# Sums of squares for two RMS norms: from transposed tiles with GpSimd additions to rows with a ScalarE row sum

## The chip, the cores and the metric

The kernel runs on one core of a Trainium2 chip. The metric is the device time of one execution in microseconds, as the median of three runs. A profile of one execution shows the engines: PE (TensorE, matmuls; its weight loads are shown apart as PEld), DVE (VectorE), ACT (ScalarE), POOL (GpSimd) and SP (SyncE, which here only issues DMAs; its queue is written SPq).

## The reference, cut to what matters

One layer of a hybrid decoder block. The input `x` (512 tokens x 2048) is normalised and projected; the columns of the projection feed an S5 scan, a differential attention and a cross-attention into 256 memory tokens, which are normalised too. All three are gated, concatenated, projected, normalised and added to `x`.

```python
def rmsnorm(x, g):
    var = jnp.mean(x32 * x32, axis=-1, keepdims=True)
    return (x32 * lax.rsqrt(var + NORM_EPS) * g).astype(x.dtype)

h = rmsnorm(x, norm_pre[l])
proj = h @ w_in[l]                    # 2048 x 5120
u_s, g_s, q_d, k_d, v_d, g_d, q_x, g_x = jnp.split(proj, split_at, axis=-1)
...
mem_n = rmsnorm(mem, norm_mem[l])
kv = mem_n @ w_mem_kv
```

The change concerns the two `mean(x32 * x32)`: of the 512 rows of `x` and of the 256 rows of `mem`.

## The kernel before, in words

All weights come in chunks of 128 x 1024 numbers (512 KB). The matmuls run in a split form: each operand is a high part (`hi`, a rounded copy made on ACT) and a low part (`lo`, the difference, made on DVE), and each product takes three matmuls (`mm3`). For a chunk, `load` (line 110) issues the DMA into one of three `raw` buffers, `parts` (line 124) makes `whi` on ACT and `wlo` on DVE into one of two buffers each, and the chunk's function then issues 24 or more matmuls in four portions. The main loop (from line 1090) does, for chunk n: load chunk n + 2, split chunk n + 1, run the matmuls of chunk n.

Between the four portions of each chunk the loop calls what is registered for that place: `at_slot(n, f)` puts `f` behind a quarter of chunk n, so slot 6.25 is behind the first portion of chunk 7. Everything outside the weight products is placed with it. PE's instructions keep the order of the program (`pin`). On the other engines and on SP's queue a list scheduler may let a later instruction pass an earlier one that cannot start yet; from chunk 9 on, ACT and DVE work is kept behind the latest weight split (`After`, `marks`).

Chunks 0 to 7 are the first four column tiles of u (the S5 input), with the contraction running over chunks, so that the transposed input can arrive in pieces: chunk c uses k = 2c and 2c + 1. `h_pair(k)` (line 308) loads 128 x 2 x 512 numbers of x transposed (`xT`, three buffers), and makes the scaled high part `hhi` on ACT and the low part `hlo` on DVE. `h_square(k)` (line 321) squares the same `xT` on ACT, and for all but the first, adds the squares to `xss` on POOL (line 327). A fold on POOL (line 360) leaves 128 x 512. `column_scale` (line 161) sums that over the partitions with tiny matmuls against ones, and `rsqrt_mean` (line 157) turns the sums into `rcol`, one scale for each token with the tokens on partitions: a DVE multiply-add and a power on POOL (line 159). `row_broadcast` (line 169) makes four diagonal matrices on DVE and four matmuls on PE, and a copy puts the scale for every partition into `rb`. The outputs of u are multiplied by it (`evac_u`, tile `ut`), which frees the accumulators that chunk 8 needs.

The memory follows the same way at chunks 8 to 19: `mem_load` and `mem_split` make `mhi` and `mlo` from transposed `mem`, `mem_square` (line 276) squares on ACT and adds into `macc` on POOL (line 282), `mem_stats` folds twice (lines 285 and 286), `column_scale` gives `rm`, and `row_broadcast` gives `rmb`.

In the same stretch other work shares DVE and POOL: `discretise` (many small DVE operations on tiles `sm`, `tw`, `pwr`, `npwi`, `w`), `rotary_tables` (`posf`, `rtmp`), `diff_lambda` (`lp`), and `s5_products`, whose products `bp`, `pm` and `dp` run on POOL (lines 575 to 578) and DVE and are then used by PE in `s5_maps` and `s5_weights` (transposes at line 99, small matmuls into `ps_t`). Most instructions of ACT, DVE and SP carry line 71, that of the helper that records them, so they are told apart by their tiles.

Of the kernel before, what the change touches and what calls it, by code (L numbers as in the profile page):

```python
# [10 lines left out]
F32 = mybir.dt.float32  # L11
# [8 lines left out]
P = 128  # L20
# [34 lines left out]
def tile_hybrid_block(ctx: ExitStack, tc: tile.TileContext, a: dict, out: bass.AP):  # L55
# [5 lines left out]
    class After:  # L61
        """An engine whose instructions stay behind the latest split of a weight chunk."""

# [31 lines left out]
    def mm(*args, **kw):  # L95
        pin(pe.matmul(*args, **kw))  # L96
# [63 lines left out]

    def column_scale(col, sq, n):
        """(mean + eps)^-1/2 of the columns of sq, with the columns on partitions."""
        sp_ = psum("t")
        w = sq.shape[-1] // P
        for j in range(w):
            mm(sp_[:, j:j + 1], sq[:, j * P:(j + 1) * P], ones[:, 0:1], start=True, stop=True)
        rsqrt_mean(col, sp_[:, :w], n)

    def row_broadcast(dst, r, n, pool):
# [36 lines left out]
    def add_cols(src, js, rhs, nk, evac, n=SEQ):  # L206
        """Column tiles js of a product with the columns on partitions."""
        acc = {}
        nc_ = nk // 8
        for c in range(nc_):  # L210
            for i, j in enumerate(js):
                def f(wh, wl, c=c, i=i, j=j):
                    if c == 0:
                        acc[j] = psum("mm")
                    for kk in range(8):
                        k = c * 8 + kk
                        sl = slice(kk * P, (kk + 1) * P)
                        rh, rl = rhs(k)
                        mm3(acc[j][:, :n], wh[:, sl], wl[:, sl], rh, rl, k == 0, k == nk - 1)
                        if kk in (1, 3, 5):  # L220
                            yield
                    if c == nc_ - 1:
                        evac(i, acc[j])
                    yield
                chunks.append((src[j, c], f))

    def add_rows(src, nt, lhs, order, evac, tag="mm"):
        """A product with the tokens on partitions, 512 columns."""
        acc = {}
# [20 lines left out]

    # ------------------------------------------------------------ memory keys and values
    s5stack, mstack, hstack, prstack = ExitStack(), ExitStack(), ExitStack(), ExitStack()
# [4 lines left out]
    mlo = mp.tile([P, NK, NMEM], F32R, name="mlo")  # L257
    macc = mp.tile([P, 4, NMEM], F32, name="macc")
    rmb = mp.tile([P, NMEM], F32, name="rmb")
# [15 lines left out]

    def mem_square(i4):
        if i4 == 0:
            s.activation(macc, mem_raw[0], AF.Square)
        else:
            msq = mp.tile([P, 4, NMEM], F32, tag="sq", name="msq", bufs=2)  # L280
            s.activation(msq, mem_raw[i4], AF.Square)
            g.tensor_tensor(macc, macc, msq, ALU.add)

    def mem_stats():
        g.tensor_tensor(macc[:, 0:2, :], macc[:, 0:2, :], macc[:, 2:4, :], ALU.add)
        g.tensor_tensor(macc[:, 0, :], macc[:, 0, :], macc[:, 1, :], ALU.add)

# [15 lines left out]

    # ------------------------------------------------------------ h^T and the token scale
    xss = xp_.tile([P, 2, SEQ], F32, name="xss")
    h_raw = {}
# [13 lines left out]

    def h_square(k):
        if k == 0:
            s.activation(xss, h_raw[k], AF.Square)
        else:
            sq = mp.tile([P, 2, SEQ], F32, tag="sq", name="sq", bufs=2)
            s.activation(sq, h_raw[k], AF.Square)
            g.tensor_tensor(xss, xss, sq, ALU.add)

    def h_scales():
        v.tensor_scalar(r05, rcol, 0.5, None, ALU.mult)  # L330
        v.tensor_scalar(r04, rcol, 0.5 * (1.0 - LAMBDA_INIT), None, ALU.mult)

    # ------------------------------------------------------------ u
    def evac_u(j, acc):
# [21 lines left out]
    for i, n in enumerate((0, 0.75, 1.5, 2.25, 3, 3.75)):  # L356
        at_slot(n, lambda k=2 * i + 4: h_pair(k))
        at_slot(n + 0.25, lambda k=2 * i: h_square(k))
    at_slot(4.5, lambda: h_square(12))
    at_slot(4.75, lambda: (h_square(14), g.tensor_tensor(xss[:, 0, :], xss[:, 0, :], xss[:, 1, :], ALU.add)))  # L360
    at_slot(5.5, lambda: column_scale(rcol, xss[:, 0, :], D))
    at_slot(6.25, lambda: row_broadcast(rb, rcol, NT, mp))
    at_slot(10, h_scales)
    for i in range(4):
        at_slot(8.5 + 2 * i, lambda i=i: (mem_load(i), mem_split(i), mem_square(i)))
    at_slot(15.5, mem_stats)
    at_slot(17, lambda: column_scale(rm, macc[:, 0, :], D))
    at_slot(19, lambda: row_broadcast(rmb, rm, 2, mp))

# [4 lines left out]

    # ------------------------------------------------------------ gates and memory queries, kept in DRAM
    def evac_to(dst):
# [12 lines left out]

    # ------------------------------------------------------------ parameters of the S5 group  # L390
    s5 = {}
# [52 lines left out]
    def cmul(dst, src, n, by):  # L444
        """Powers dst.. (n of them) as the powers src.. times the power by."""
        d_, x_ = slice(dst, dst + n), slice(src, src + n)
# [9 lines left out]
    def discretise():  # L456
        """abar = exp(lambda dt) and its powers 0 to 4, (abar - 1) / lambda times the powers 0 to 3;
        with the signs that the stacked real and imaginary halves of a group want."""
        dtt = exact_exp(ldt, "dt")
# [46 lines left out]
        v.tensor_scalar(npwi, npwi, -1.0, None, ALU.mult)  # L506
        # abar^4, with a pair of groups on the partitions: magnitude, and turns negated
        r_, f_, tmp = small(), small(), small()
# [36 lines left out]

    # ------------------------------------------------------------ S5: what depends on the parameters alone, kept in DRAM
    pre = {}
# [12 lines left out]
    def s5_products(o):  # L560
        """B with the powers 0 to 3 and (abar - 1) / lambda, C with the powers 0 to 4; real parts of a group
        on the lower half of the partitions, imaginary ones on the upper half."""
        bc = pt("bc", [512], 2)
# [29 lines left out]
    def s5_weights(o):  # L593
        """Direct kernels of the lags 0 to 3 (D on lag 0)."""
        bp, dp, kz = pre["bp", o], pre["dp", o], pre["kz"][o % 2]
# [10 lines left out]

    # ------------------------------------------------------------ S5
    def s5_open():
# [17 lines left out]
    def s5_load(o):  # L626
        """Maps and output maps of an octet of groups."""
        sp = t512("sp", 2, (P, 1152))
# [3 lines left out]
    def s5_u(i, x):  # L632
        """u of two octets, the first or the second groups of their pairs."""
        if x == 0:
# [9 lines left out]
    def s5_toeplitz(i, x):  # L644
        """The direct kernels of two octets as Toeplitz blocks."""
        tm = s5["d"][i % 2]["tm"]
# [5 lines left out]
    def s5_angles(o):  # L652
        """Cosines and sines of the turns of abar^4 at each chunk."""
        cs = t512("cs", 2, (P, 2, 4, P))
# [17 lines left out]
    def s5_states(o):  # L672
        """The states at the end of a chunk, in steps: turned back, summed, turned forward, spread over the groups."""
        x, ub, us, (c_, s_) = s5["d"][o % 2]["x"], s5["ub"], oct_[o]["us"], oct_[o]["cs"]
# [34 lines left out]
    def s5_outputs(o):  # L709
        """y, and twice its GELU"""  # L710
        d, us = s5["d"][o % 2], oct_[o]["us"]
# [53 lines left out]

    # ------------------------------------------------------------ GLU of the S5 group
    S1 = len(chunks)
# [35 lines left out]

    # ------------------------------------------------------------ memory attention, beside v and g_d
    S2 = len(chunks)
# [88 lines left out]

    # ------------------------------------------------------------ differential attention
    S3 = len(chunks)
# [19 lines left out]
    def evac_k(h, acc):  # L916
        """The keys of either map, on both halves of the partitions."""
        t1_, t2_ = rotary(acc)
# [9 lines left out]
    def evac_q(h, acc):  # L928
        """Of either map, the high parts on one half of the partitions and the low parts on the other."""
        t1_, t2_ = rotary(acc)  # L930
# [71 lines left out]

    # ------------------------------------------------------------ output projection, post norm, residual
    S4 = len(chunks)
# [36 lines left out]

    # the last 512 columns: four chunks as before, four kept for a pass by token tiles; the last tile in halves
    pieces = [(tt, c0, w) for tt, c0, w in ((0, 0, 512), (1, 0, 512), (2, 0, 512), (3, 0, 256), (3, 256, 256))]
# [37 lines left out]

    # ------------------------------------------------------------ the program
    for i in range(9):
# [131 lines left out]
```

## Time and profile before

| | |
|---|---|
| time, median of 3 runs (lowest, highest) | 843.36 us (842.02, 843.72) |
| span of the profiled execution | 843.7 us (the page gives no other time for it) |
| PE busy | 813.4 us (96%), 4042 matmuls |
| PEld busy | 672.5 us (80%) |
| DVE busy | 563.3 us (67%) |
| ACT busy | 351.7 us (42%) |
| POOL busy | 105.1 us (12%), 87 instructions |
| DMA | 125.32 MB, mean 149 GB/s |

The page cuts the span into 40 slices of 21.1 us; a digit is the busy share of an engine in a slice in tenths. A timeline row gives the start, the duration, the engine, the operation with its output and inputs, the count if several were merged, and in brackets how long the engine was idle before it and what ended that. A row of groups gives the count, the busy time and the mean in ns. A matmul's duration overlaps the next one's, so PE's pace is read from starts, not from durations.

### The profile page before, as it was taken

To read this page: it belongs to the slowest core of one execution; us is meant where nothing else is said; L and a number is where in the kernel's file an instruction comes from. 1 tells how busy PE (TensorE), PEld (TensorE's weight loads), DVE (VectorE), ACT (ScalarE), POOL (GpSimd) and SP (SyncE) were. 2 spreads that over 40 slices of the span, in tenths; PEclk is the share of its full clock that TensorE was granted. 3 is DMA by queue.
4 is the path that set the end of the run, shared out by engine and by line. 5 is a ranking of instruction groups with operands and counts; after the bars stand their busy time and mean duration, and the time that the engine had idled before them with its cause. 6 is when DMAs were issued, how large, how long until landed. Compare 5 with 4: busy or idle time off the path is not lost.

```text
span 843.7 us, 10965 instructions
## 1 busy us (share of the span) xinstructions
PE 813.4 (96%) x4042; PEld 672.5 (80%) x4042; DVE 563.3 (67%) x1001; ACT 351.7 (42%) x589; POOL 105.1 (12%) x87
## 2 busy tenths in 40 slices
PE   8797978998999999999999999999999999999996
PEld 6686768887878788878888888888888888888885
DVE  5998798646788888885675455557988943232335
ACT  7522442433353544424334353445767633131321
POOL 2703564630000000000000000000100010000000
PEclk9998988999999999999999999999999999999998
DMA  8444545883645555427656322222223426222226
GB/s 293 159 177 135 202 139 193 263 266 97 183 117 162 164 146 170 118 100 237 212 174 236 104 88 75 88 88 93 82 76 111 140 79 221 100 100 99 96 105 249
DMA packets 59494, 125.32 MB, mean 149 GB/s; under 512 B 12592, under 2 KB 26032, under 8 KB 59312
## 3 DMA queue, kind: packets, MB, share of 16 engines
q1 hardware_dynamic: 59440, 124.61, 44.9%
q8 instruction: 32, 0.52, 0.3%
q14 instruction: 22, 0.18, 0.1%
HBM read 103.22 MB, written 21.36 MB: 148 GB/s over the span
## 4 chain that ended last, share of the span: by engine, by line
PE 78%; DVE 12%; DMA 4%; issue 3%; ACT 2%; SPq 1%; POOL 0%; DVEq 0%; POOLq 0%; ACTq 0%
PE ps_mm L96 65%; PE ps_s L96 7%; PE ps_t L96 4%; DMA raw<-in_w_in_a_dram 2%; DVE wlo L71 2%; DVE sm L71 2%; DVE hlo L71 2%; PE ps_t L99 1%; DVE mlo L71 1%; DMA sp<-sp_dr 1%; SPq L71 1%; DVE x L71 1%; DVE ra L71 1%; ACT whi L71 1%; DVE ut L71 1%
## 5 line engine op out<-in xcount | busy, mean ns | idle before, releaser
L71 DVE TENSOR_TENSOR wlo<-raw,whi 128x1024 fp32r<-128x1024 f32 (+1 forms) x135 | 168.6, 1250 | 174.9 <-ACT whi L71 174.2
L71 ACT CAST whi<-raw 128x1024 fp32r<-128x1024 f32 (+1 forms) x135 | 139.0, 1030 | 326.4 <-PE ps_mm L96 214.2
L96 PE MATMUL ps_mm<-hhi,wlo 128*128 128x512 f32 x512 | 202.5, 395 | 8.8 <-DVE wlo L71 8.8
L96 PE MATMUL ps_mm<-hhi,whi 128*128 128x512 f32 x512 | 204.6, 400 | 0.3 <-DVE ut L71 0.3
L96 PE MATMUL ps_mm<-hlo,whi 128*128 128x512 f32 x512 | 202.5, 396 | 1.7 <-DVE hlo L71 1.7
L96 PEld LDWEIGHTS ps_mm<-hhi,wlo 128*128 128x128 f32 x512 | 97.9, 191 | 30.5 <-DVE wlo L71 9.6
L96 PEld LDWEIGHTS ps_mm<-hlo,whi 128*128 128x128 f32 x512 | 97.9, 191 | 22.5 <-DVE hlo L71 3.1
L96 PEld LDWEIGHTS ps_mm<-hhi,whi 128*128 128x128 f32 x512 | 98.0, 191 | 21.1 <-DVE ut L71 0.7
L159 POOL TENSOR_TENSOR so<-so,neghalf 128x1 f32<-128x1 f32 x16 | 11.6, 724 | 355.4 <-DVE so L71 327.4
L96 PE MATMUL ps_mm<-whi,hhi 128*128 128x512 f32 x128 | 49.9, 390 | 0.0
L96 PE MATMUL ps_mm<-whi,hlo 128*128 128x512 f32 x128 | 49.9, 390 | 0.0
L96 PE MATMUL ps_mm<-wlo,hhi 128*128 128x512 f32 x128 | 49.9, 390 | 0.0
L96 PE MATMUL ps_mm<-whi,yshi 128*128 128x512 f32 (+1 forms) x112 | 43.9, 392 | 0.0
L96 PE MATMUL ps_mm<-wlo,yshi 128*128 128x512 f32 (+1 forms) x112 | 43.3, 387 | 0.0
L96 PE MATMUL ps_mm<-whi,yslo 128*128 128x512 f32 (+1 forms) x112 | 43.3, 386 | 0.0
L96 PEld LDWEIGHTS ps_mm<-whi,hlo 128*128 128x128 f32 x128 | 24.0, 188 | 5.1
L96 PEld LDWEIGHTS ps_mm<-whi,hhi 128*128 128x128 f32 x128 | 24.1, 188 | 4.7
L96 PEld LDWEIGHTS ps_mm<-wlo,hhi 128*128 128x128 f32 x128 | 24.0, 188 | 4.8
L71 DVE SCALAR_TENSOR_TENSOR hlo<-xT,cols,hhi 128x512 fp32r<-128x512 f32 x16 | 25.1, 1610 | 2.9 <-ACT hhi L71 2.9
L71 DVE TENSOR_TENSOR x<-ra 64x512 f32<-64x512 f32 x32 | 26.3, 822 | 0.8
L656 POOL TENSOR_TENSOR cs<-cst,ftn 128x512 f32<-128x512 f32 x8 | 9.2, 1159 | 135.9 <-DVE ra L71 135.9
L71 ACT ACTIVATE pr<-sm,nm 128x128 f32<-128x128 f32 (+3 forms) x32 | 18.0, 564 | 18.8 <-DVE nm L71 18.7
(333 smaller groups left out, 1515.8 us busy)
## 6 DMA issues: line engine op xcount, KB each, us to landing
raw<-in_w_in_a_dram SPq DMA_DIRECT2D x63, 512.0 KB, 3.9
raw<-in_w_out_b_dram SPq DMA_DIRECT2D x32, 512.0 KB, 3.2
raw<-in_w_in_b_dram SPq DMA_DIRECT2D x16, 512.0 KB, 3.2
sp<-sp_dr SPq DMA_DIRECT2D x8, 576.0 KB, 4.5
raw<-in_w_kv_a_dram SPq DMA_DIRECT2D x8, 512.0 KB, 3.4
raw<-in_w_kv_b_dram SPq DMA_DIRECT2D x8, 512.0 KB, 4.6
raw<-in_w_glu_a_dram SPq DMA_DIRECT2D x8, 512.0 KB, 4.1
xT<-in_xT_dram SPq DMA_DIRECT2D x7, 512.0 KB, 6.5
```

The lines of the kernel that those rows point to most:

```text
L71: r = f(*args, **kw)
L96: pin(pe.matmul(*args, **kw))
L99: pin(pe.transpose(o, i, ident))
L159: g.tensor_tensor(dst, dst, neghalf.to_broadcast([P, dst.shape[-1]]), ALU.pow)
L656: g.tensor_tensor(an, iota.unsqueeze(1).to_broadcast([P, 4, P]), ftn[:, 4 * o:4 * o + 4].unsqueeze(2).to_broadcast([P, 4, P]), ALU.mult)
```

## The change

`x` and `mem` are loaded a second time, as they lie: 128 rows of 2048 numbers at a time (1 MB), four times for `x` and twice for `mem`, into two new buffers `rows`. ACT squares each in place, and its accumulator gives the sum of each row in a column of `ssq`. The squares of the transposed tiles, the additions and folds on POOL with their tiles `xss`, `macc`, `sq` and `msq`, and `column_scale` with its matmuls are removed. `rsqrt_mean` now reads `ssq`. The row squares of `x` are registered at slots 3.5, 4.25, 5 and 5.75, those of `mem` at 9.5 and 11.5; `rsqrt_mean` of `x` moves from slot 5.5 to 6; `row_broadcast` stays. The diff, without the hunks that only drop comments:

```diff
-    def column_scale(col, sq, n):
-        sp_ = psum("t")
-        w = sq.shape[-1] // P
-        for j in range(w):
-            mm(sp_[:, j:j + 1], sq[:, j * P:(j + 1) * P], ones[:, 0:1], start=True, stop=True)
-        rsqrt_mean(col, sp_[:, :w], n)
...
-    macc = mp.tile([P, 4, NMEM], F32, name="macc")
...
-    def mem_square(i4):
-        if i4 == 0:
-            s.activation(macc, mem_raw[0], AF.Square)
-        else:
-            msq = mp.tile([P, 4, NMEM], F32, tag="sq", name="msq", bufs=2)
-            s.activation(msq, mem_raw[i4], AF.Square)
-            g.tensor_tensor(macc, macc, msq, ALU.add)
-
-    def mem_stats():
-        g.tensor_tensor(macc[:, 0:2, :], macc[:, 0:2, :], macc[:, 2:4, :], ALU.add)
-        g.tensor_tensor(macc[:, 0, :], macc[:, 0, :], macc[:, 1, :], ALU.add)
+    ssq = mp.tile([P, NT + 2], F32, name="ssq")
+
+    def row_square(src, i):
+        xr = mp.tile([P, D], F32, tag="rows", name="rows", bufs=2)
+        sy.dma_start(xr, src)
+        s.activation(xr, xr, AF.Square, accum_out=ssq[:, i:i + 1])
...
-    xss = xp_.tile([P, 2, SEQ], F32, name="xss")
...
-    def h_square(k):
-        if k == 0:
-            s.activation(xss, h_raw[k], AF.Square)
-        else:
-            sq = mp.tile([P, 2, SEQ], F32, tag="sq", name="sq", bufs=2)
-            s.activation(sq, h_raw[k], AF.Square)
-            g.tensor_tensor(xss, xss, sq, ALU.add)
...
     for i, n in enumerate((0, 0.75, 1.5, 2.25, 3, 3.75)):
         at_slot(n, lambda k=2 * i + 4: h_pair(k))
-        at_slot(n + 0.25, lambda k=2 * i: h_square(k))
-    at_slot(4.5, lambda: h_square(12))
-    at_slot(4.75, lambda: (h_square(14), g.tensor_tensor(xss[:, 0, :], xss[:, 0, :], xss[:, 1, :], ALU.add)))
-    at_slot(5.5, lambda: column_scale(rcol, xss[:, 0, :], D))
+    for tt in range(NT):
+        at_slot(3.5 + 0.75 * tt, lambda tt=tt: row_square(a["x"][tt * P:(tt + 1) * P], tt))
+    at_slot(6, lambda: rsqrt_mean(rcol, ssq[:, 0:NT], D))
     at_slot(6.25, lambda: row_broadcast(rb, rcol, NT, mp))
     at_slot(10, h_scales)
     for i in range(4):
-        at_slot(8.5 + 2 * i, lambda i=i: (mem_load(i), mem_split(i), mem_square(i)))
-    at_slot(15.5, mem_stats)
-    at_slot(17, lambda: column_scale(rm, macc[:, 0, :], D))
+        at_slot(8.5 + 2 * i, lambda i=i: (mem_load(i), mem_split(i)))
+    for b_ in range(2):
+        at_slot(9.5 + 2 * b_, lambda b_=b_: row_square(a["mem"][b_ * P:(b_ + 1) * P], NT + b_))
+    at_slot(17, lambda: rsqrt_mean(rm, ssq[:, NT:], D))
     at_slot(19, lambda: row_broadcast(rmb, rm, 2, mp))
```

## The prediction

> **What bounds the kernel now.** I read the page's slices first, then PE's own timeline for its idle gaps, then DVE, GpSimd (POOL), ScalarE (ACT) and the SyncE queue (SPq) in those places.
>
> ```profile
> span 843.7 us, 10965 instructions
> ...
> PE   8797978998999999999999999999999999999996
> ...
> DVE  5998798646788888885675455557988943232335
> ...
> POOL 2703564630000000000000000000100010000000
> ```
>
> A slice is 21.1 us. After slice 10 PE is at 9 or more nearly throughout; its holes lie in the first seven slices, the ones in which DVE is fullest and the only ones in which POOL works much. So what this change can move lies before 150 us. After that PE runs its matmuls end to end, and time won earlier should stay won. PE's idle gaps there, and the pace that PE keeps where nothing is late (the last row, from the chain of waits: 144 matmuls in 32.65 us, 0.227 us each, 5.44 us for a chunk of 24):
>
> ```profile
> 20.35 0.50 PE L96 MATMUL ps_mm<-hlo,whi 128*128 128x512 f32 x1 [1.15 <-DVE hlo L71]
> ...
> 40.92 0.80 PE L96 MATMUL ps_mm<-hhi,wlo 128*128 128x512 f32 x1 [4.41 <-DVE wlo L71]
> ...
> 44.57 0.39 PE L96 MATMUL ps_mm<-hhi,wlo 128*128 128x512 f32 x1
> ...
> 76.77 0.80 PE L96 MATMUL ps_mm<-hhi,wlo 128*128 128x512 f32 x1 [4.37 <-DVE wlo L71]
> ...
> 82.12 0.39 PE L96 MATMUL ps_mm<-hhi,whi 128*128 128x512 f32 x1
> ...
> 109.94 1.11 PE L99 MATMUL ps_t<-cst,bp 128*128 128x128 f32 x4 [2.97 <-POOL bp L577]
> 110.71 0.77 PE L96 MATMUL ps_mm<-hhi,whi 128*128 128x512 f32 x1
> ...
> 115.55 0.53 PE L96 MATMUL ps_mm<-hhi,wlo 128*128 128x512 f32 x1
> ...
> 125.93 0.59 PE L96 MATMUL ps_t<-dp,bp 128*32 128x64 f32 x16 [1.88 <-DVE dp L71]
> ...
> 545.38 32.65 PE ps_mm L96 x144
> ```
>
> Columns are start, duration, instruction, and in brackets the idle time before it and who ended it. All but one gap ends with DVE. A long gap is paid twice, because PE is slow after it: from 40.92 to 44.57 there are nine matmul steps, 3.65 us instead of 9 x 0.227 = 2.04, so 1.6 us more; from 76.77 to 82.12 thirteen steps, 5.35 instead of 2.95, 2.4 more; from 110.71 to 115.55 eleven, 4.84 instead of 2.50, 2.3 more. Why is DVE late?
>
> ```profile
> 4.98 0.75 DVE L71 SCALAR_TENSOR_TENSOR hlo<-xT,cols,hhi 128x512 fp32r<-128x512 f32 x1 [2.33 <-ACT hhi L71]
> ...
> 29.45 10.18 DVE L71 SCALAR_TENSOR_TENSOR hlo<-xT,cols,hhi 128x512 fp32r<-128x512 f32 x4
> 39.55 0.18 DVE L71 TENSOR_SCALAR sm<-par 128x64 f32<-128x64 f32 x1
> 39.65 1.21 DVE L71 TENSOR_TENSOR wlo<-raw,whi 128x1024 fp32r<-128x1024 f32 x1
> ...
> 28.37 9.04 POOL L327 TENSOR_TENSOR xss<-xss,sq 128x1024 f32<-128x1024 f32 x3 [1.20 <-ACT sq L71]
> ...
> L71 DVE SCALAR_TENSOR_TENSOR hlo<-xT,cols,hhi 128x512 fp32r<-128x512 f32 x16 | 25.1, 1610 | 2.9 <-ACT hhi L71 2.9
> ```
>
> An hlo takes 0.75 us where POOL is quiet and 2.55 each (10.18 / 4) while POOL runs the three xss additions from 28.37 to 37.41. The wlo of chunk 5 is queued behind those four and starts at 39.65; PE waits for it until 40.92. Over all 16 the mean is 1610 ns: 25.1 us instead of 16 x 0.75 = 12.0. The additions that this change removes hold DVE up by 13.1 us, on a DVE that is full:
>
> ```profile
> 30.00:40.00 10.00, 6.51 (x29) 5.07 (x27) 10.00 (x6) 5.33 (x7) 9.08 (x6) 1.00 0.46 154
> 40.00:50.00 10.00, 9.08 (x33) 7.40 (x34) 9.59 (x47) 2.34 (x2) 0.00 (x0) 0.83 0.47 170
> ...
> 75.49 1.22 DVE L71 TENSOR_TENSOR wlo<-raw,whi 128x1024 fp32r<-128x1024 f32 x1
> ```
>
> (Windows of 10 us: busy PE, PEld, DVE, ACT, POOL, then granted clock, DMA share and GB/s.) DVE is busy 10.00 and 9.59 of 10; ACT has room (5.33 and 2.34), DMA is under half.
>
> **The change part by part.** Term A, the seven xss additions and the fold leave POOL. The hlo fall to 0.75 us and the gaps ahead of 20.35 and 40.92 should close. 1.15 + 4.41 + 1.6 of slow matmuls = 7.2 us, all on PE's path. What is late next there is the cast and split of the next chunk: ACT's whi and DVE's wlo (1.21) take some 2.3 us together and have a 5.44 us chunk to do it in, so nothing. Bounds: 1.15 (only the first gap) to 7.2; I take 7.2, since both gaps end behind an hlo or a wlo queued directly behind contended hlo.
>
> Term B, the tiny matmuls of column_scale leave PE's pinned order:
>
> ```profile
> 50.24 0.95 PE L96 MATMUL ps_t<-ones,xss 128*128 128x1 f32 x8
> ...
> 55.28 1.05 PE L96 MATMUL ps_t<-diag,ones 128*128 128x128 f32 x8
> ...
> 133.73 0.50 PE L96 MATMUL ps_t<-ones,macc 128*128 128x1 f32 x4
> ...
> L71 ACT ACTIVATE sq<-xT 128x1024 f32<-128x1024 f32 x7 | 7.3, 1046 | 0.0
> ...
> L71 ACT ACTIVATION_READ_ACCUMULATOR ojk<-ps_mm 128x1 f32 x16 | 3.1, 194 | 0.0
> ```
>
> 0.95 + 0.50 = 1.4 us. The scale now reads the accumulated column directly; row_broadcast (55.28) keeps its place.
>
> ACT: twelve squares of 1024 at 1.05 us leave (12.6 us). Six of 2048 come; none is in the trace, so I take twice the 1024 row as the top and once as the bottom, plus the accumulator read of 0.19: between 1.2 and 2.3, six of them 7 to 14 us. I take the top, since twice the elements is nearest to twice the row. That is ACT unchanged within 2 us, covered by its idle time above; with that cover gone it would be 1.3 us. It also frees each xT buffer one square (1.05 us) sooner.
>
> DMA: six loads of 1 MB are new, four of them ahead of the row_broadcast, and SPq carries them in order.
>
> ```profile
> DMA  0779999999540988850009542058017415700017
> GB/s 9 220 245 303 336 385 395 380 370 369 173 176 16 328 260 275 270 219 4 0 18 356 215 170 92 0 201 321 11 35 306 183 75 185 268 0 0 0 35 283
> ...
> xT<-in_xT_dram SPq DMA_DIRECT2D x7, 512.0 KB, 6.5
> ...
> 16.86 0.38 SPq L71 DMA_DIRECT2D raw<-in_w_in_a_dram  x1
> 20.36 4.93 SPq L71 DMA_DIRECT2D xT<-in_xT_dram  x2
> 25.34 0.43 SPq L71 DMA_DIRECT2D raw<-in_w_in_a_dram  x1
> ```
>
> (Forty slices of 2 us, 0 to 80.) From 6 to 20 us the engines are full at 370 to 395 GB/s; from 20 to 42 they move about 175 GB/s, so there is room for 4 MB at 20 us and none at 10. Where do the loads go? The queue kept the order of the program this far (the raw of 16.86 is chunk 5's, then xT 10 and 12, then chunk 6's raw), and the first row load stands behind chunk 6's raw. Once hlo is fast, the raw of 25.34 no longer stands behind a blocked xT, and row 0 can issue near 21 us, row 1 near 26 (behind chunk 7's raw), row 2 when square 0 is done, near 30, row 3 near 33. A load takes between 2.7 us (1.05 MB at 395 GB/s) and 13 (twice the 6.5 of a 512 KB load in the crowded stretch); at about 5, row 3 is there by 38, squared by 41, and POOL's power (1.0) and four diagonals (0.9) end near 43. PE gets to the row_broadcast at 55.28 - 7.2 - 0.95 = 47.1. Cost 0, with 4 us to spare; at the 13 us end row 3 lands near 54 (rows 2 and 3 each a load later) and PE loses 12. I take 0, as the traffic after 20 us is half of what made the 6.5. The raw loads behind the rows in SPq have slack: the one issued at 16.86 is split at 39.65. The two mem rows come at chunks 10 to 12 and their scale is used at chunk 19: 0.
>
> Term C, the gap ahead of 76.77. DVE runs the S5 parameter arithmetic among the wlo, full, and chunk 10's wlo (75.49) comes late. Its queue is 13.1 us shorter, PE arrives 7.2 + 0.95 = 8.2 us sooner: DVE gains 4.9 on PE, and the gap is 4.37. So it could close whole, 4.37 + 2.4 = 6.8; if DVE spends the freed time waiting for loads and casts, nothing. I take three quarters, 5.0, because the hlo must still wait for their loads in the crowded first 20 us.
>
> Term D, the mem additions.
>
> ```profile
> 76.63 1.66 DVE L71 SCALAR_TENSOR_TENSOR mlo<-mT,cols,mhi 128x256 fp32r<-128x256 f32 x4
> ...
> 99.11 4.82 DVE L71 SCALAR_TENSOR_TENSOR mlo<-mT,cols,mhi 128x256 fp32r<-128x256 f32 x4
> ...
> 99.83 2.41 POOL L282 TENSOR_TENSOR macc<-macc,msq 128x1024 f32<-128x1024 f32 x1 [1.73 <-ACT msq L71]
> ...
> 120.50 2.58 POOL L282 TENSOR_TENSOR macc<-macc,msq 128x1024 f32<-128x1024 f32 x1
> ...
> 120.75 2.49 DVE L71 TENSOR_TENSOR lp<-lv 128x128 f32<-128x128 f32 x1
> ```
>
> Four mlo take 1.66 alone and 4.82 here; about two thirds of that excess runs beside the macc addition, 2 us. The rotary work queued behind them holds POOL's bp, and so the gap of 2.97 at 109.94: minus 2.0 and its 2.3 of slow matmuls. The lp (2.49 beside the macc addition of 120.50) stands ahead of the dp that ends the gap of 1.88. All together 6.2 us; the S5 products stay on POOL and block DVE as well, so the bottom is 0. I take half, 3.0. Here a rule counts: by the Trainium skill (TensorE: Matmul & The Clock Gate, Part 1: The HAM clock gate) the clock falls after an idle window of about 3.4 us. The gap of 2.97 is shorter, yet 2.3 us of slow matmuls follow it, so the trace does not bear the threshold out as a minimum gap; by the rule those 2.3 us would not be this gap's, and the forecast would be 1.2 us longer.
>
> Sum: 7.2 + 1.4 + 5.0 + 3.0 = 16.6. The profiled span is 843.7, 0.04% over the median of 843.36; 843.4 - 16.6 = 826.8.
>
> **The rivals.** (1) The gain stops at A and B: DVE stays the limit from 40 to 136 us and the gaps of C and D return at PE's new pace. For it: DVE at 9.59 of 10 with no POOL at all. Against: the queue is 13.1 us shorter. 843.4 - 8.6 = 834.8. (2) Slower: the row squares wait in ACT's queue behind a weight cast, which itself waits for PE to free its buffer, and the next row load waits for that square. Each such round is a chunk, 5.44 us. One for each of the four rows puts the scale at 43 + 21.8 = 64.8, PE waits 17.7 and pays 2.4 of slow matmuls: 20.1 against 16.6, 846.9. With three it is still faster (14.7 lost); so it decides from the fourth. For it: in-order queues. Against: two buffers let two rows pass in one round, and ACT is half idle. (3) The additions are not what slows the hlo: then only B remains, 842.0. Against it: 0.75 against 2.55 us, changing with POOL. (4) C and D come whole and more, DVE being no limit up to 136 us: 7.2 + 1.4 + 6.8 + 6.2 = 21.6 and beyond, 822 down to 817.
>
> **How the numbers follow.** Forecast (A, B and most of C and D) 0.62, rival 1 0.17, rival 4 0.10, rival 2 0.06, rival 3 0.05. Less than 0.2% (1.7 us) can hardly be told from no change. Faster 0.62 + 0.17 + 0.10 = 0.89, same 0.05, slower 0.06. The forecast's own range is 820 to 833 (C and D from 1.8 to all). The range to hold 8 in 10 takes in rival 1 and a row wait of 3 us with it, 838, and half of rival 4, 819.
>
> **What would show it.** Right: hlo mean near 750 ns; no idle before PE at chunk 2 and 5; row_broadcast's matmuls near 47 us with no wait for rcol; DVE no longer full from 20 to 40; wlo of chunk 10 without a PE gap. Wrong: PE idle ahead of ps_t<-diag, released by DVE diag; a raw or xT wait ended by DMA before 45 us; the gap near 77 still there, about 68; a new gap behind POOL's bp.

## The result, and the profile after

| | before | after |
|---|---|---|
| median, both kernels timed together, 4 runs each (lowest, highest) | 843.54 us (842.02, 844.89) | 834.18 us (831.94, 836.21) |
| ratio after / before, 95% interval | | 0.9887 (0.9862 to 0.9912) |
| span of the profiled execution | 843.7 us | 834.4 us |

The change makes the kernel 1.1% faster, 9.3 us on the spans (9.4 on the medians) where 16.6 were forecast. A span is that of one execution, and executions of the same kernel lie up to 8 us apart; where spans are compared below, the ratios or medians are given beside them. The ratios leave out three executions that were far slower than all others (1251 and 3628 us of the kernel before, 1613 of a changed one). The page of the kernel after, the busy sums and the same three rows of slices (20.9 us each) as before:

```profile
PE 808.6 (97%) x4030; PEld 668.6 (80%) x4030; DVE 542.9 (65%) x1001; ACT 351.8 (42%) x589; POOL 73.6 (9%) x74
...
PE   8978989989999999999999999999999999999996
...
DVE  4778796638987888865774544557988843232335
...
POOL 0003453520000000000000000000101010000000
```

POOL lost 31.5 us (105.1 to 73.6) and DVE 20.4 (563.3 to 542.9); ACT is unchanged. POOL's first three slices show 0 now. PE's timeline after, its gaps and the marks that answer to those of before:

```profile
13.28 0.50 PE L96 MATMUL ps_mm<-hhi,whi 128*128 128x512 f32 x1 [1.02 <-ACT hhi L71]
...
53.73 2.05 PE L96 MATMUL ps_t<-diag,ones 128*128 128x128 f32 x8 [5.40 <-DVE diag L71]
...
74.70 0.50 PE L96 MATMUL ps_mm<-hhi,wlo 128*128 128x512 f32 x1 [2.20 <-DVE wlo L71]
...
82.82 0.60 PE L99 MATMUL ps_t<-cst,bp 128*128 128x128 f32 x4
...
104.31 0.66 PE L99 MATMUL ps_t<-cst,bp 128*128 128x128 f32 x4
...
117.29 0.43 PE L96 MATMUL ps_t<-dp,bp 128*32 128x64 f32 x16 [1.25 <-DVE dp L71]
...
120.49 0.58 PE L96 MATMUL ps_mm<-mhi,wlo 128*128 128x256 f32 x1 [2.34 <-DVE wlo L71]
```

The gaps of 1.15, 4.41 and 2.97 us of before are gone, that of 1.88 is 1.25, the one ahead of chunk 10's `wlo` product is halved, and a new one of 5.40 stands ahead of the diagonal matmuls of `row_broadcast`. The same instruction in both traces gives a running account:

| mark on PE | before | after | gained so far |
|---|---|---|---|
| ready for `row_broadcast` (after: 53.73 - 5.40) | 55.28 | 48.33 | 6.95 |
| its diagonal matmuls start | 55.28 | 53.73 | 1.55 |
| chunk 10's first `wlo` product | 76.77 | 74.70 | 2.07 |
| first `ps_t<-cst,bp` | 85.53 | 82.82 | 2.71 |
| the `ps_t<-cst,bp` behind the 2.97 gap | 109.94 | 104.31 | 5.63 |
| the `ps_t<-dp,bp` behind the 1.88 gap | 125.93 | 117.29 | 8.64 |
| first `mhi,wlo` product behind it | 129.54 | 120.49 | 9.05 |
| end of the span | 843.7 | 834.4 | 9.3 |

So nearly 7 us are won by 48 us, 5.4 of them are given back at once to a wait for the scale of the rows, and the rest is won later. Why is the scale late? First ACT, then SPq, then the tile `rows` by itself (duration in ns, least, median and largest):

```profile
46.78 1.05 ACT L71 CAST whi<-raw 128x1024 fp32r<-128x1024 f32 x1 [2.48 <-PE ps_mm L96]
47.85 1.28 ACT L71 ACT_TABLE_LOAD   x1
...
49.84 1.89 ACT L71 ACTIVATE rows<-rows 128x2048 f32<-128x2048 f32 x1
51.64 0.19 ACT L71 ACTIVATION_READ_ACCUMULATOR rows<-rows 128x1 f32 x1
```

```profile
24.10 0.50 SPq L71 DMA_DIRECT2D rows<-in_x_dram  x1
...
25.12 0.62 SPq L71 DMA_DIRECT2D par<-in_par_dram  x1
...
27.79 6.20 SPq L71 DMA_DIRECT2D rows<-in_x_dram  x2
...
39.32 0.33 SPq L71 DMA_DIRECT2D rows<-in_x_dram  x1
```

```profile
L71 ACT ACTIVATE rows<-rows x4: 1894/1916/1921, 31.6 to 49.8; 128x2048 f32<-128x2048 f32 x4
...
DMA to landing us min/median/max: 5.0/6.1/9.5
```

The last row load is issued only at 39.32, since it needs the buffer that square 1 frees. It lands 5.1 us later, near 44.4. Its square stands behind the cast of chunk 8's weights, which waits 2.48 us for PE to free its buffer, and behind a table load and three small activations; it starts at 49.84, 5.4 us after the landing. From its end (51.83) the scale takes `rcol`, POOL's power and the diagonals, and PE starts at 53.73. The windows of 10 us (columns as before) show the loads:

```profile
30.00:40.00 10.00, 10.00 (x45) 8.26 (x44) 6.56 (x23) 7.36 (x8) 0.00 (x0) 1.00 1.01 399
...
60.00:70.00 10.00, 10.00 (x46) 8.27 (x45) 9.90 (x26) 3.71 (x6) 3.42 (x3) 1.00 0.84 303
70.00:80.00 10.00, 7.80 (x28) 5.96 (x27) 9.84 (x15) 2.95 (x3) 3.27 (x3) 0.83 0.44 161
```

From 30 to 40 us the DMA engines are full (1.01, 399 GB/s, against 0.46 and 154 before). DVE, at 10.00 from 30 to 40 before, now has idle time there (6.56), and is full at 9.90 and 9.84 from 60 to 80, where chunk 10 still waits. The freed time lies early and the work late. The S5 parameter arithmetic, a long chain of small DVE operations, starts with the landing of `par`:

```profile
33.24 0.20 DVE L71 TENSOR_SCALAR sm<-par 128x64 f32<-128x64 f32 x1 [0.46 <-DMA par<-in_par_dram]
```

`par` is small but issued two places behind the first row load, at 25.12, and it lands 8.1 us later. In the kernel before it was issued at 28.83 and landed 3.1 us later; there its first use, at 39.55, stood behind `hlo` and not behind the load.

### The profile page after: what moved, and what is told of

It reads as the page before. It is cut to its first block, busy times and chain, and to the rows that moved or that the text cites. A ratio compares the mean times of both kernels' runs of the same rounds, so it can differ in the third digit from the quotient of the medians.

```text
span 834.4 us, 10930 instructions
## 1 busy us (share of the span) xinstructions
PE 808.6 (97%) x4030; PEld 668.6 (80%) x4030; DVE 542.9 (65%) x1001; ACT 351.8 (42%) x589; POOL 73.6 (9%) x74
## 4 chain that ended last, share of the span: by engine, by line
PE 78%; DVE 9%; DMA 6%; issue 3%; ACT 3%; SPq 1%; POOL 0%; DVEq 0%; POOLq 0%; ACTq 0%
PE ps_mm L96 67%; PE ps_s L96 6%; PE ps_t L96 4%; DMA raw<-in_w_in_a_dram 3%; DVE wlo L71 2%; PE ps_t L99 1%; SPq L71 1%; ACT whi L71 1%; DMA sp<-sp_dr 1%; DVE sm L71 1%; DVE ra L71 1%; DVE x L71 1%; DMA mk_dr<-mk 1%; DVE mlo L71 1%; ACT L71 1%
## 5 line engine op out<-in xcount | busy, mean ns | idle before, releaser
L96 PE MATMUL ps_mm<-gehi,whi 128*128 128x512 f32 x64 | 25.2, 394 | 0.0
L96 PE MATMUL ps_mm<-gehi,wlo 128*128 128x512 f32 x64 | 25.1, 392 | 0.0
```

## The experiments

Each time is a ratio to the kernel before on the same chip, with its 95% interval, the median, and the profiled span.

**The two halves.** One kernel takes `x` by rows and keeps the old way for `mem` (`macc` and `msq` live in the buffers of `rows`); the other takes `mem` by rows and keeps `h_square` for `x`.

```diff
 # x by rows only
-        at_slot(8.5 + 2 * i, lambda i=i: (mem_load(i), mem_split(i)))
-        at_slot(9.5 + 2 * b_, ... row_square(a["mem"]...))
+        at_slot(8.5 + 2 * i, lambda i=i: (mem_load(i), mem_split(i), mem_square(i)))
+    at_slot(15.5, mem_stats)
...
 # mem by rows only
-    for tt in range(NT):
-        at_slot(3.5 + 0.75 * tt, ... row_square(a["x"]...))
+        at_slot(n + 0.25, lambda k=2 * i: h_square(k))
...
+    at_slot(5.5, lambda: column_scale(rcol, xss[:, 0, :], D))
```

> Rows for x only; mem keeps its squares of the transposed tiles, its additions on POOL and its column_scale. After the whole change the marks that PE passes in both profiles lie 2.7 us earlier at the first S5 transposes (82.8 against 85.5) and 8.6 us earlier at the fourth set of kernel matmuls (117.3 against 125.9), so most of the gain seems to come from the memory stage. Theory 1 (the mem additions block DVE and so PE there): this kernel gains about 2.5 to 3.5 us only, 840 to 841. Theory 2 (the memory stage gains because x's change shortened DVE's queue before it): it keeps most of the gain, 834 to 836.

> Rows for mem only; x keeps its squares, additions on POOL and column_scale. Theory 1: gains the memory stage's part, about 6 us, 837 to 838. Theory 2: gains 0 to 2 us, 841.5 to 843.5. Both: the gap of PE ahead of 40.9 and the hlo of 1.6 us mean are as before the change.

`x` only: 0.9958 (0.9941 to 0.9975), 841.38 us, span 839.9. `mem` only: 0.9927 (0.9904 to 0.9951), 838.69 us, span 838.0. Both came within 1 us of theory 1. By the ratios the two save 0.42% and 0.73%, 1.15% together, against 1.13% for the whole change: within the intervals they simply add up. By the middle values the smaller part of the change, two loads instead of four, brings more; the two intervals overlap a little. Rows of PE and DVE from the timeline with `x` only, then with `mem` only:

```profile
53.65 2.04 PE L96 MATMUL ps_t<-diag,ones 128*128 128x128 f32 x8 [5.41 <-DVE diag L71]
...
95.98 4.83 DVE L71 SCALAR_TENSOR_TENSOR mlo<-mT,cols,mhi 128x256 fp32r<-128x256 f32 x4
...
106.83 0.66 PE L99 MATMUL ps_t<-cst,bp 128*128 128x128 f32 x4 [2.98 <-POOL bp L577]
```

```profile
41.73 0.50 PE L96 MATMUL ps_mm<-hhi,wlo 128*128 128x512 f32 x1 [4.41 <-DVE wlo L71]
...
77.60 0.79 PE L96 MATMUL ps_mm<-hhi,wlo 128*128 128x512 f32 x1 [4.39 <-DVE wlo L71]
...
99.61 1.67 DVE L71 SCALAR_TENSOR_TENSOR mlo<-mT,cols,mhi 128x256 fp32r<-128x256 f32 x4
```

With `x` only the wait for the scale (5.41) is there and the gap of 2.98 behind POOL's `bp` is back, with the four `mlo` at 4.83 us. With `mem` only the `mlo` take 1.67, no gap stands near 110 us, and the early gaps of 4.41 and 4.39 are as before. The wait for the scale belongs to the four row loads of `x`, the late gain to the `mem` additions.

**What the row loads of x cost.** One kernel registers the row squares a chunk earlier; the other leaves out the loads and squares of `x` altogether and sets `ssq` to a constant, so that its scale of `x` is not computed.

```diff
 # rows earlier
-        at_slot(3.5 + 0.75 * tt, ... row_square(...))
+        at_slot(2.5 + 0.75 * tt, ... row_square(...))
 # no rows of x
-    for tt in range(NT):
-        at_slot(3.5 + 0.75 * tt, ... row_square(...))
+    v.memset(ssq[:, 0:NT], float(D))
```

> The changed kernel with x's row squares registered one chunk earlier (slots 2.5, 3.25, 4, 4.75). In the changed kernel PE waits 5.4 us for the scale and runs slow for some us after it, because square 3 runs at 49.84, behind a weight cast that waited for PE and behind the sines. Theory 1 (this wait is what kept terms A and B from reaching the end): square 3 moves ahead of the cast of chunk 7, the wait goes, PE is 5 to 7 us earlier at the end: 827 to 829. Theory 2 (DVE's S5 parameter work is the limit behind it and PE would wait there instead, ahead of chunk 10's wlo): the gap moves to about 70 us and the time is 832 to 834.

> The changed kernel without the four row loads and squares of x; the sums of squares of x are a constant, so this leaves out that part of the computation. It is the bound for any way of making the sums that costs nothing on DMA, ACT and POOL. Theory 1: no wait for the scale, 826 to 828. Theory 2: 831 to 833 with a gap ahead of chunk 10's wlo. The difference to the run with early rows is what the 4 MB of loads cost: theory 1 says under 2 us.

Rows earlier: 0.9902 (0.9876 to 0.9927), 836.72 us, no better than the change as it is; theory 1 had 827 to 829, and theory 2 832 to 834 with the gap moved to chunk 10. Rows of SPq, DVE and PE from its timeline:

```profile
29.52 0.48 SPq L71 DMA_DIRECT2D par<-in_par_dram  x1
...
40.74 0.19 DVE L71 TENSOR_SCALAR sm<-par 128x64 f32<-128x64 f32 x1
...
50.50 2.05 PE L96 MATMUL ps_t<-diag,ones 128*128 128x128 f32 x8 [2.26 <-DVE diag L71]
...
79.95 0.80 PE L96 MATMUL ps_mm<-hhi,wlo 128*128 128x512 f32 x1 [5.87 <-DVE wlo L71]
```

The wait for the scale falls from 5.40 to 2.26, but `par`, now behind more rows in SPq, is issued at 29.52 and used at 40.74 instead of 33.24 (it landed after 7.3 us, near 36.8; then DVE still waited for ACT's `hhi`), and the gap ahead of chunk 10 grows from 2.20 to 5.87. What is won at one place is paid at the other. Without the rows of `x`: 0.9760 (0.9737 to 0.9784), 824.3 us, span 822.5, below the 826 to 828 of theory 1. Its PE:

```profile
47.82 1.05 PE L96 MATMUL ps_t<-diag,ones 128*128 128x128 f32 x8
...
66.08 0.50 PE L96 MATMUL ps_mm<-hhi,wlo 128*128 128x512 f32 x1 [1.75 <-DVE wlo L71]
```

There is no wait at `row_broadcast`, and chunk 10's gap is 1.75. So 4 MB of loads with their four squares and the wait for them, which the forecast had at nothing, cost 834.4 - 822.5 = 11.9 us of span, or 10.7 by the ratios (0.9887 less 0.9760). 8.6 of it is there at chunk 10's `wlo` product (74.70 against 66.08). Against the run with earlier rows they cost 836.72 - 824.30 = 12.4 us, where theory 1 had under 2; it took what stands behind the rows as free.

**The cause of the slow hlo, and what bounds chunk 10.** The kernel before, without the ten full additions into `xss` and `macc` on POOL (its sums of squares are incomplete), and beside it on the same chip the changed kernel once more. The edit of the first, against the kernel before:

```diff
-            g.tensor_tensor(macc, macc, msq, ALU.add)
...
-            g.tensor_tensor(xss, xss, sq, ALU.add)
```

> The kernel before without the ten additions of squares on POOL (seven for x, three for mem); squares on ACT, folds and column_scale stay and work on the first squares alone, so this leaves out most of the two sums. No row loads. If the additions on POOL hold DVE up: hlo mean near 750 ns instead of 1610, no gap of PE ahead of 41 us, and 823 to 828 (as the run without row loads of x, which lacks also the tiny matmuls, plus 1). If it is the squares on ACT or the xT buffers they hold that make the hlo late: hlo stay above 1.2 us and the time within 2 us of before.

> The changed kernel once more beside the two moves, for a comparison on the same chip: 833 to 836, a ratio of 0.987 to 0.991 to the kernel before.

No additions: 0.9853 (0.9833 to 0.9872), 831.07 us, span 829.3. After again: 0.9905 (0.9881 to 0.9929), 835.67 us. The `hlo` without additions (in the changed kernel they are the same, 743/747/754 ns), then PE of the kernel without additions:

```profile
L71 DVE SCALAR_TENSOR_TENSOR hlo<-xT,cols,hhi x16: 744/748/754, 5.0 to 32.7; 128x512 fp32r<-128x512 f32 x16
```

```profile
48.46 1.05 PE L96 MATMUL ps_t<-diag,ones 128*128 128x128 f32 x8
...
69.98 0.80 PE L96 MATMUL ps_mm<-hhi,wlo 128*128 128x512 f32 x1 [5.02 <-DVE wlo L71]
```

All sixteen `hlo` take 0.75 us, where the mean was 1.61: the additions alone were what slowed them. By the Trainium skill (SBUF — State Buffer, "Who interferes with whom") a DVE instruction with two inputs in SBUF contends with a GpSimd instruction that reads SBUF, since its second input comes through a port that the two share. The pairs here agree: 0.75 against 2.55 us for an `hlo`, 1.67 against 4.83 for four `mlo`; the port itself no run here shows. PE reaches `row_broadcast` at 48.46 without a wait. But the gap ahead of chunk 10 does not close; it is 5.02. PE comes to it 7.4 us sooner than in the kernel before (64.96 against 72.40), but the `wlo` only some 7 (DVE starts it at 68.29 instead of 75.49), although the S5 arithmetic starts at 29.85 instead of 39.55. The time missed what was expected, 823 to 828, by 3 us; this gap is more than that. On this chip the additions were worth 843.47 - 831.07 = 12.4 us to the kernel before and the change 843.47 - 835.67 = 7.8, so that about a third is given back.

**par earlier.** `par` and `dsk` are loaded at slot 0.5 instead of 4: on the changed kernel, on the changed kernel with earlier rows, and on the kernel before.

```diff
-    at_slot(4, lambda: (sy.dma_start(par, a["par"]), sy.dma_start(dsk, a["dsk"])))
+    at_slot(0.5, lambda: (sy.dma_start(par, a["par"]), sy.dma_start(dsk, a["dsk"])))
```

> The changed kernel with one thing moved: the loads of the S5 parameters par and dsk (104 KB) are issued behind slot 0.5 instead of slot 4, where they stood behind row 0 on SPq and landed 8.1 us after issue, at 33.2. Theory 1 (the loads that the rows push back start DVE's S5 arithmetic late, and DVE idles in 20 to 33): DVE starts it before 25, the sines run before square 1 and no longer stand ahead of square 3, the gap of 2.2 us ahead of chunk 10's wlo goes, the wait for the scale shrinks from 5.4 to 2 to 4 us: 827 to 831. Theory 2 (only the arrival of row 3 counts): wait for the scale and time as in the changed kernel, 833 to 835.

> Both moves together: row squares one chunk earlier and par and dsk behind slot 0.5. With early rows alone the wait for the scale fell to 2.26 us, but par landed late behind the rows, DVE's S5 arithmetic began near 40 us and PE waited 5.87 us ahead of chunk 10's wlo. Theory 1: with par early both gaps shrink to under 2 us, 825 to 828, near the 824.3 of the run without row loads. Theory 2 (the 4 MB cost their DMA time whatever the order): 832 to 835.

> The kernel before with par and dsk issued behind slot 0.5. Theory 1 (in the kernel before DVE is full from 16 to 40 us with hlo held up by the additions, so an early par finds no room): 842 to 844, no change. Theory 2 (an early par is worth the same 5 us in any version, and has nothing to do with the change): 837 to 839.

On the changed kernel: 0.9835 (0.9812 to 0.9858), 829.22 us, span 827.2. Rows of DVE and PE from its timeline, and its window from 20 to 30 us:

```profile
17.55 0.19 DVE L71 TENSOR_SCALAR sm<-par 128x64 f32<-128x64 f32 x1
...
51.61 2.05 PE L96 MATMUL ps_t<-diag,ones 128*128 128x128 f32 x8 [4.52 <-DVE diag L71]
```

```profile
20.00:30.00 10.00, 10.00 (x46) 8.29 (x45) 9.79 (x33) 6.41 (x10) 0.00 (x0) 1.00 0.87 292
```

The S5 arithmetic starts at 17.55, DVE is full from 20 to 30, and no gap stands ahead of chunk 10 any more. So an early `par` closes that gap, as was said. The wait for the scale shrank only to 4.52, not to 2 to 4: the last square ends at 48.5, and `rcol`, queued on DVE behind S5 operations, starts at 49.87. With earlier rows as well: 0.9835 (0.9814 to 0.9857), 829.37 us. Both theories missed this one: the wait for the scale is still 3.29, and a new gap of 1.75 at 13.91 ends with ACT's `hhi`. On the kernel before the same edit gains nothing: 1.0020 (1.0006 to 1.0034), 845.94 us. DVE has no free time there, and PE's gap only moves, from chunk 10 to 1.98, 1.40 and 2.34 us ahead of 48 us and 3.43 at 69.58. The early DVE time is worth something only once the additions are gone, and then only if work is there to fill it.

The start of the S5 arithmetic is not all that sets the gap. Its last operations ahead of chunk 10's `wlo`, first in the changed kernel, where POOL makes the S5 products `bp`, `dp` and `pm` beside them (POOL, then DVE), then with `par` early, where POOL is quiet:

```profile
65.74 1.69 POOL L553 TENSOR_TENSOR bp<-w,bc 128x512 f32<-128x512 f32 x1 [12.48 <-DVE w L71]
...
66.44 1.18 DVE L71 TENSOR_SCALAR pwr<-pwr,cst 128x320 f32<-128x320 f32 x1
...
67.88 1.40 DVE L71 TENSOR_SCALAR npwi<-npwi 128x320 f32<-128x320 f32 x1
```

```profile
46.52 0.37 DVE L71 TENSOR_SCALAR pwr<-pwr,cst 128x320 f32<-128x320 f32 x1
...
48.29 0.31 DVE L71 TENSOR_SCALAR npwi<-npwi 128x320 f32<-128x320 f32 x1
```

From this `pwr` to the end of the arithmetic DVE takes 7.0 us (66.44 to the start of the `wlo` at 73.42) instead of 2.2 (46.52 to 49.87, less 1.1 for a `wlo` in between). The one operation that falls between two products, `w` at 69.20, takes 0.34 us in both kernels. So the products that stay on POOL seem to stretch DVE's work as the additions did, and by more than the gap of 2.20. How much of the gap is theirs is not measured, as no run took the products away. Without the rows of `x`, too, the S5 arithmetic starts no sooner than in the changed kernel (33.67), and yet chunk 10 comes 8.6 us sooner.

**The broadcast later.** `row_broadcast` of `x` at slot 6.75 instead of 6.25, so that PE has two more portions of chunk 7 ahead of the scale: on the changed kernel, and together with the early `par` (run twice).

```diff
-    at_slot(6.25, lambda: row_broadcast(rb, rcol, NT, mp))
+    at_slot(6.75, lambda: row_broadcast(rb, rcol, NT, mp))
```

> The changed kernel with row_broadcast behind slot 6.75 alone. Theory 1: the gap ahead of the broadcast falls from 5.4 to about 2.7 us, but DVE's S5 arithmetic is as late as in the changed kernel and its wlo of chunk 10 takes back most of it: 832 to 834. Theory 2 (the wait for the scale alone is what costs): 829 to 831.

> The changed kernel with par and dsk early and, besides, row_broadcast behind slot 6.75 instead of 6.25, so that PE has twelve more matmuls (2.7 us) of chunk 7 ahead of it. With par early alone the gap ahead of ps_t<-diag was 4.52 us and the 18 matmuls behind it ran slow. Theory 1 (the wait for the scale is a late arrival, and PE had work that did not need it): the gap falls to about 1.8 us, chunk 8 starts 3 to 4 us sooner, 825 to 827. Theory 2 (the wait only moves behind the broadcast, to chunk 8's accumulators, which need ut): the same 829 with a gap released by DVE ut.

> The kernel with par and dsk early and the broadcast behind slot 6.75 once more, for its profile. Theory 1: PE's gap ahead of ps_t<-diag is 1 to 2.5 us, no gap ahead of chunk 10's wlo, the fourth set of kernel matmuls starts near 108 us (111.7 with par early alone, 117.3 in the changed kernel): 824 to 827. Theory 2: a new gap released by DVE ut at chunk 8 takes the gain back.

Alone: 0.9830 (0.9809 to 0.9851), 829.87 us, span 827.5. Its PE:

```profile
52.85 1.50 PE L96 MATMUL ps_t<-diag,ones 128*128 128x128 f32 x8 [2.69 <-DVE diag L71]
...
70.05 0.50 PE L96 MATMUL ps_mm<-hhi,wlo 128*128 128x512 f32 x1 [1.74 <-DVE wlo L71]
```

The wait halves, as forecast, and chunk 10 does not take it back (1.74), so the theory that it would take back most of it is wrong: DVE waits less for the scale too, and its `wlo` of chunk 10 starts at 68.77 instead of 73.42. Together with the early `par`: 0.9780 (0.9755 to 0.9805), and in the second run 0.9800 (0.9779 to 0.9821), 826.23 us, span 824.5, both as theory 1 had it. PE of the second run:

```profile
51.71 1.13 PE L96 MATMUL ps_t<-diag,ones 128*128 128x128 f32 x8 [1.77 <-DVE diag L71]
54.63 0.50 PE L96 MATMUL ps_mm<-hhi,whi 128*128 128x512 f32 x1 [0.42 <-DVE ut L71]
```

1.77 us of the wait and nothing at chunk 10 remain. This is the fastest kernel of the study that leaves nothing out, 2.0 to 2.2% ahead of the kernel before. Against the change as made (0.9887) its two ratios stand 0.0087 and 0.0107 lower, 7 to 9 us, with two slot numbers moved.

## Why the prediction was right, and where its steps failed

The direction and the mechanism held: POOL's additions were what slowed DVE, DVE was what PE waited for, and the time won stayed won. The size did not: 834.18 lies 1.2 us beyond the forecast's own range of 820 to 833, and the wide range, 819 to 838, holds it because rival 1 and a row wait of 3 us had been taken into it. Of the signs for being right, the `hlo` of 750 ns, the closed gaps at chunks 2 and 5 and a DVE with free time from 20 to 40 us came; the broadcast without a wait and chunk 10 without a gap did not, and idle time ahead of `ps_t<-diag`, a sign for being wrong, did. The single steps:

- **Terms A and B (8.6 forecast).** Right in the main: 8.15 of it lies ahead of `row_broadcast` (B's other 0.5 is at 133.73), and PE was ready there 6.95 us sooner. The missing 1.2 is mostly a new gap of 1.02 at 13.28, where chunk 1 waits for ACT's `hhi`.
- **"Cost 0, with 4 us to spare" for the row loads.** This step failed and cost 5.40 us of waiting, and 1.65 us more in slow matmuls: from the broadcast to the gap of chunk 10 PE took 18.77 us (74.70 - 2.20 - 53.73) instead of 17.12 (76.77 - 4.37 - 55.28). The forecast issued the rows at 21, 26, 30 and 33 us; they went at 24.10, 27.79, 33.6 (the second half of the merged SPq row) and 39.32. It gave each 5 us and a square at once. The second took 9.5 us to land, on DMA engines at a share of 1.01, so that its square ended and freed the buffer for the fourth at 39.3. The fourth did land in 5.1 us, near 44.4, but its square met the mechanism of rival 2: it stood behind a weight cast that waited for PE, and started 5.4 us after the landing. In the forecast's sum that mechanism cost nothing; it cost PE 5.40 us, one round of the four that the rival had counted.
- **Term C (5.0 forecast, about 2.8 measured:** 2.17 of gap and 0.64 of slow matmuls). It was sized from the length of DVE's queue, as if all 13.1 us taken out of it moved chunk 10's `wlo` forward. The kernel without additions, with as short a DVE queue, moved it by some 7 and had a gap of 5.02. What counts is when DVE gets through the S5 arithmetic ahead of that `wlo`, and the freed time lies ahead of work that cannot start yet: DVE was idle for 7.6 us between 20 and 50 (7.75, 6.56 and 8.07 busy of 10), mostly for ACT's `whi`, and 0.46 for `par`. In the kernel that closes the gap this arithmetic starts at 17.55. The bound "if DVE spends the freed time waiting for loads and casts, nothing" named this. POOL's S5 products, which seem to stretch the end of the arithmetic, were not in the term at all; their share is open.
- **Term D (3.0 forecast, 6.3 measured:** 9.05 gained by the `mhi,wlo` product at 120.49, against 2.71 at 82.82). Mis-sized: half was taken because the S5 products stay on POOL, but the whole bound of 6.2 came. The `mem`-only kernel gives 5.7 us of span for it alone, 6.2 by its ratio.
- **ACT.** The square of 2048 with its row sum takes 1.92 us and the accumulator read 0.18, close to the top that was taken. Its price was right; its place in the queue was what counted.
- **The rivals.** Rival 1's time, 834.8, is nearly the measured one, but by another path: A and B were not the whole gain, C came by half and D whole, and the rows took 7 us away. Rival 3 is ruled out by the `hlo` at 0.75 us, and rival 4 by C.
- **Slips of the working.** With C and D whole the sum gives 821.8, where the forecast's own range starts at 820; and POOL also works in slices 8 and 9 (6 and 3 tenths), not only in the first seven. Neither changes the argument.

A and B fell 1.2 short and C 2.2, and D was 3.3 over; that these cancel was luck. What is left of the miss of 7.3 us on the spans (16.6 - 9.3) is, to within 0.3, the 5.40 and 1.65 of the row loads.

## What to carry to other kernels

A load that replaces arithmetic is not free because the DMA engines have room on average: follow it to the square, the cast it stands behind, and the buffer that the next load waits for, and give each its start time. When an engine is relieved, ask when the work that could fill the gap is able to start; here a long chain of DVE work waited for a small load issued at 25.1 us, and issuing it 16 us sooner was worth 6.4 us on the changed kernel (835.67 to 829.22 on the same chip) and nothing on the kernel before. Look also where the work that is left on GpSimd falls: VectorE's operations beside it were slow here too. After a change of this kind look again at the slots around it, as the earlier order was made for other finishing times.

## What the runs showed of the hardware

**The clock fell after gaps of about 2 us.** The granted clock (last column but two) of the kernel after, behind its gap of 2.20, which ends at 74.70, and of the kernel without rows of `x`, behind its gap of 1.75, which ends at 66.08:

```profile
72.50:75.00 2.50, 0.30 (x1) 0.30 (x2) 2.47 (x4) 2.31 (x3) 0.85 (x1) 1.00 0.00 0
75.00:77.50 2.50, 2.50 (x8) 1.94 (x7) 2.50 (x6) 0.00 (x0) 0.00 (x0) 0.58 0.68 256
77.50:80.00 2.50, 2.50 (x9) 2.00 (x9) 2.45 (x5) 0.00 (x0) 0.00 (x0) 0.74 0.95 341
```

```profile
65.00:70.00 5.00, 3.92 (x17) 3.23 (x18) 5.00 (x8) 1.64 (x2) 0.00 (x0) 1.00 0.49 152
70.00:75.00 5.00, 5.00 (x26) 4.12 (x25) 4.04 (x9) 3.14 (x6) 1.06 (x1) 1.00 0.94 332
```

After 2.20 us of idle PE the clock is 0.58 and then 0.74, and the stretch to the first `ps_t<-cst,bp` takes 8.12 us; after 1.75 it stays at 1.00 and the stretch takes 6.52. So this gap is paid nearly twice, and the other not. In the second run of the changed kernel the gap there was 1.95, and the clock fell too, to 0.72 and 0.60, for a stretch of 8.14 us. The diagonal matmuls took 1.13 us behind a gap of 1.77, but 2.05 behind one of 2.26 (rows earlier), 1.50 behind 2.69 (broadcast later) and 2.05 behind 5.40. The Trainium skill (TensorE: Matmul & The Clock Gate, Part 1: The HAM clock gate) gives an idle window of about 3.4 us that runs free of the kernel. That the price does not grow with the gap would fit a free-running window, but as a least length of a gap the 3.4 us are not borne out: 2.20 and 1.95 were enough. What sets the point was not tried.

**Landing times where the DMA engines are full.** The issues of the kernel after from 20 to 40 us (KB of one, median us to landing):

```profile
par<-in_par_dram SPq DMA_DIRECT2D x1, 96.0 KB, 8.1
dsk<-in_dsk_dram SPq DMA_DIRECT2D x1, 8.0 KB, 7.6
```

96 KB took 8.1 us and 8 KB 7.6, two and three places behind a 1 MB load that took 7.5 itself. With `par` issued at 9.00, ahead of all row loads, the two took 8.0 and 7.6; from 10 to 20 us the DMA share was 1.06 there. In the kernel before, with a share of 0.57 from 20 to 30, they took 3.1 and 4.0. So the landing time followed how full the engines were, and hardly the size.
